# Down products of a Strassen FFN: other order of the PSUM sums, one kept tile W per pair of strips, splits of blocks on VectorE

## The chip, the cores and the metric

The kernel runs on one core of a Trainium2 chip. The metric is the time of one execution in device microseconds. The kernel before took 1813.65 us (median of 3 runs, 1813.53 to 1815.38).

## The reference, cut to what matters

One inference step of a decoder layer with two groups of tokens (1024 prompt tokens and 8 x 4 sample tokens, 1056 columns together) that share all weights: a block of three mixers, cross-attention, and then the part of this case, a SwiGLU feed-forward layer with 2816 hidden rows, and a last RMS norm. All values are fp32.

```
u = rmsnorm(h, W['norm_ffn'][l])
h = h + (jax.nn.silu(u @ W['w_ffn_gate'][l]) * (u @ W['w_ffn_up'][l])) @ W['w_ffn_down'][l]
...
y = rmsnorm(h, W['norm_final'])
```

The change touches only the product with `w_ffn_down`, and of its 22 blocks of 128 hidden rows the first 18. The outputs are h after the last norm, and the states of the mixers.

## The kernel before, in words

Tokens lie along the free dimension: a feature block is a tile of 128 partitions x 1056 columns, cut in two halves of 528 (TH), and each of these in two parts c of 264 (HB). A product in fp32 is made of three matmuls: each operand is split into a rounded high part and the rest (hi, lo), and hi·hi, hi·lo and lo·hi are summed in PSUM (L1323 to L1325). ScalarE makes hi by a copy, another engine makes lo by a subtraction.

The three feed-forward products go by a Strassen-Winograd scheme with 7 products instead of 8 (table `PRODUCTS`, L1281; function `strassen`, L1328). The weight side of a product comes from `lefts` (L1221): per pair of output strips, GpSimd makes the sums s1 and s3 (L1244, L1245) and VectorE s2 and s4 (L1246, L1247), and `split_left` splits seven blocks (hi on ScalarE, L1259; lo on VectorE, L1260, tile `wlo`). The right side are the blocks B11, B21, B22, T1 to T4 of the hidden rows. They were written to DRAM by the stage before (`keep`, L1417) and are read back and split by `load_right` (L1359, tile `xd`): hi on ScalarE (L1369), lo on VectorE for two blocks of three and on GpSimd for the third (L1370).

The down product runs over 3 groups g of 6 hidden blocks, and within a group over 4 pairs m of output strips. Each (g, m) has seven products i = 0 to 6, each of 2 parts x 3 blocks x 3 = 18 matmuls. A PSUM tile `st` holds both parts and there are three of them; a (g, m) uses four in turn: G0 takes B11 (i = 0) and then also B21 (i = 2), G1 takes T2 (1) and T3 (3), G2 takes T1 (4) and B22 (6), G3 takes T4 (5). After a product the function `down` (L1543) takes the sum so far out of PSUM: i = 0 is copied by ScalarE into a half of a tile `tm` (L1547), 1 and 3 are added to it by VectorE (L1549, L1554), 2, 4, 5 and 6 are added straight into h (L1552, L1558, L1560, L1562). GpSimd adds the sums in `tm` to h12 (after 1, L1550), h22 and h21 (after 3, L1555, L1556). A later product that goes into the same PSUM tile has to wait until the reader before it is done.

The 63 blocks of the right side do not come evenly. `feed` (L1405) loads and splits 23 of them around the last products of the stage before, and then 3 after each product of m = 3, for the next group; the split stands three products (6 ticks) later in the program. In group 2, and from the last of m = 3 in group 1 on, `feed` brings the operands of the last four hidden blocks instead (`hl`, L1389; `wd`, L1400).

TensorE's and SyncE's work stands in the order of the program. That of VectorE, ScalarE and GpSimd is put in order by the scheduler, which goes by its own costs; each engine then works through its list in order, so an instruction waits for those ahead of it too.

Of the kernel before, what the change touches and what calls it, by code (L numbers as in the profile page):

```python
# [26 lines left out]
NG, GK = 3, 3  # L27
# [32 lines left out]
def hybrid_step(ctx, tc, xT, memT, consts_d, masks_d, wbd_d, poolw_d, spool_d, w_kv, w_xbc, w_dt, w_lg, w_pool, w_z, h0_d,  # L60
# [1252 lines left out]
    ps_ = ExitStack()  # L1313
    ps = ps_.enter_context(tc.tile_pool(name="ps2", bufs=2, space=PSUM, reuse_waits="tile"))

    def product(i, w, G, c, kk, k0=0):
        xb, g, begins = PRODUCTS[i]
        whi, wlo = w
        for k in range(kk):
            a, b = k * P, k * P + P  # L1320
            xh, xl = X[xb, k0 + k, c]
            out = G[g][:, c, :HB]
            nc.tensor.matmul(out, whi[:, a:b], xh, start=begins and k == 0, stop=False, skip_group_check=True)  # L1323
            nc.tensor.matmul(out, whi[:, a:b], xl, start=False, stop=False, skip_group_check=True)  # L1324
            nc.tensor.matmul(out, wlo[:, a:b], xh, start=False, stop=k == kk - 1, skip_group_check=True)  # L1325
        tick()

    def strassen(kk, after, by_part=False, k0=0):  # L1328

        G = {}  # L1330
        if by_part:
# [8 lines left out]
                G = {}  # L1340
            return
        for i in range(7):
            g = PRODUCTS[i][1]
            if g not in G:
                G[g] = ps.tile([P, 2, 512], F32, tag="st", name=nm("st"), bufs=3)
            w = block()
            for c in range(2):
                product(i, w, G, c, kk, k0)
            after(i, slice(0, 2), G)

    def temps():
# [7 lines left out]
    def load_right(wait):  # L1359
        b, f = next(rights)  # L1360
        t = slot(F32R, "xd")
        hi, lo = t[:, :TH], t[:, TH:]
        nc.sync.dma_start(lo.bitcast(F32), hid_dram[:, f, NB8.index(b)])
        eng = nc.gpsimd if len(hids) % 3 == 2 else nc.vector
        hids.append(t)

        def split():
            yield wait
            nc.scalar.activation(hi, lo.bitcast(F32), AF.Copy)  # L1369
            eng.tensor_tensor(lo, lo.bitcast(F32), hi.bitcast(F32), op=OP.subtract)  # L1370
            for c in range(2):
                X[b, 4 + f, c] = hi[:, c * HB:(c + 1) * HB], lo[:, c * HB:(c + 1) * HB]

        spawn(split())
# [153 lines left out]
        spawn(keep(f, ga, (v22, v12, v21, v11)))  # L1528


    for g in range(NG):
        for m in range(4):
            if g == 0 and m < 3:
# [1 line left out]
                    load_h(i)  # L1535
            if (g, m) == (0, 0):
                feed(2)
            t = slot(name="tm")
            u3, u2 = [t[:, i * TH:(i + 1) * TH].rearrange("p (c t) -> p c t", c=2) for i in range(2)]
            (h11, h12), (h21, h22) = [[x[:, i * TH:(i + 1) * TH].rearrange("p (c t) -> p c t", c=2) for i in range(2)]  # L1540
                                      for x in h[2 * m:2 * m + 2]]

            def down(i, cs, G):  # L1543
                at = lambda g: G[g][:, cs, :HB]
                vec, gp = nc.vector.tensor_tensor, nc.gpsimd.tensor_tensor
                if i == 0:
                    nc.scalar.activation(u3, at(0), AF.Copy)  # L1547
                elif i == 1:
                    vec(u2, u3, at(1), op=add)  # L1549
                    gp(h12, h12, u2, op=add)  # L1550
                elif i == 2:
                    vec(h11, h11, at(0), op=add)  # L1552
                elif i == 3:
                    vec(u3, u3, at(1), op=add)  # L1554
                    gp(h22, h22, u3, op=add)  # L1555
                    gp(h21, h21, u3, op=add)  # L1556
                elif i == 4:
                    vec(h22, h22, at(2), op=add)  # L1558
                elif i == 5:
                    vec(h21, h21, at(3), op=add)  # L1560
                else:
                    vec(h12, h12, at(2), op=add)  # L1562
                if m == 3:
                    feed(3)

            strassen(GK, down, k0=4 + g * GK)
    while tail:
        spawn(tail.pop(0)())
    drain()
# [161 lines left out]
```

## Time and profile before

| what | value |
|---|---|
| median of 3 runs | 1813.65 us |
| time of the profiled execution | 1811.17 us |
| its span in the profile | 1809.3 us |
| TensorE busy | 1727.7 us (95%) |
| VectorE busy | 1181.0 us (65%) |
| ScalarE busy | 780.8 us (43%) |
| GpSimd busy | 704.7 us (39%) |

The span is the stretch from the first to the last recorded instruction; the execution is 1.9 us longer. The down products lie from about 1525 to 1744 us after the span's start. Shares are means over stages with different limits, so the rows below are taken from that stage alone.

### The profile page before, as it was taken

To read this page: it belongs to the slowest core of one execution; us is meant where nothing else is said; L and a number is where in the kernel's file an instruction comes from. 1 tells how busy PE (TensorE), PEld (TensorE's weight loads), DVE (VectorE), ACT (ScalarE), POOL (GpSimd) and SP (SyncE) were. 2 spreads that over 40 slices of the span, in tenths; PEclk is the share of its full clock that TensorE was granted. 3 is DMA by queue.
4 is the path that set the end of the run, shared out by engine and by line. 5 is a ranking of instruction groups with operands and counts; after the bars stand their busy time and mean duration, and the time that the engine had idled before them with its cause. 6 is when DMAs were issued, how large, how long until landed. Compare 5 with 4: busy or idle time off the path is not lost.

```text
span 1809.3 us, 31919 instructions
## 1 busy us (share of the span) xinstructions
PE 1727.7 (95%) x12307; PEld 1674.3 (93%) x12307; DVE 1181.0 (65%) x2112; ACT 780.8 (43%) x1533; POOL 704.7 (39%) x695
## 2 busy tenths in 40 slices
PE   8899999999999999999999999999999998989897
PEld 7798988888999999999999989999999998989896
DVE  5888997788753534455566488555555557798755
ACT  6544544467744213345564364322222224244244
POOL 2423556665342322211221243433344424465534
PEclk9999999999999999999999999999999999999998
DMA  9111222241230522243344232222222237245122
GB/s 345 62 55 60 67 67 87 95 148 61 101 111 32 207 83 84 78 144 124 116 139 146 95 131 72 103 93 95 90 90 101 92 110 264 91 153 166 32 83 97
DMA packets 106504, 197.52 MB, mean 109 GB/s; under 512 B 15344, under 2 KB 33392, under 8 KB 106352
## 3 DMA queue, kind: packets, MB, share of 16 engines
q1 hardware_dynamic: 94832, 173.54, 28.4%
q10 hardware_dynamic: 11520, 21.94, 3.3%
q8 instruction: 97, 1.59, 0.4%
q14 instruction: 55, 0.45, 0.1%
HBM read 151.54 MB, written 43.89 MB: 108 GB/s over the span
## 4 chain that ended last, share of the span: by engine, by line
PE 76%; DVE 12%; issue 4%; POOL 3%; DMA 2%; ACT 2%; ACTq 0%; SPq 0%; DVEq 0%; POOLq 0%
PE mm L153 11%; PE mm L155 11%; PE mm L154 11%; PE st L1323 10%; PE st L1324 10%; PE st L1325 10%; DVE cy L504 2%; DVE wlo L1260 1%; PE poa L1083 1%; DVE xd L1370 1%; PE pss L1065 1%; POOL seg L576 1%; DVE x L331 1%; PE st L1452 1%; PE st L1453 1%
## 5 line engine op out<-in xcount | busy, mean ns | idle before, releaser
L1323 PE MATMUL st<-x,whi 128*128 128x264 f32 x1120 | 319.0, 285 | 3.0 <-DVE tm L1512 1.9
L153 PE MATMUL mm<-uh,whi 128*128 128x352 f32 x960 | 320.7, 334 | 0.0
L1324 PE MATMUL st<-x,whi 128*128 128x264 f32 x1120 | 318.1, 284 | 0.0
L1325 PE MATMUL st<-x,wlo 128*128 128x264 f32 x1120 | 318.0, 284 | 0.0
L155 PE MATMUL mm<-uh,wlo 128*128 128x352 f32 x960 | 310.8, 324 | 0.0
L154 PE MATMUL mm<-ul,whi 128*128 128x352 f32 x960 | 310.8, 324 | 0.0
L1323 PEld LDWEIGHTS st<-x,whi 128*128 128x128 f32 x1120 | 210.7, 188 | 3.6 <-DVE tm L1512 2.1
L1325 PEld LDWEIGHTS st<-x,wlo 128*128 128x128 f32 x1120 | 210.7, 188 | 0.0
L1324 PEld LDWEIGHTS st<-x,whi 128*128 128x128 f32 x1120 | 210.6, 188 | 0.0
L153 PEld LDWEIGHTS mm<-uh,whi 128*128 128x128 f32 x960 | 181.7, 189 | 4.5 <-issue 2.2
L154 PEld LDWEIGHTS mm<-ul,whi 128*128 128x128 f32 x960 | 182.2, 190 | 2.5
L155 PEld LDWEIGHTS mm<-uh,wlo 128*128 128x128 f32 x960 | 181.5, 189 | 0.0
L1323 PE MATMUL st<-xd,whi 128*128 128x264 f32 x504 | 148.5, 295 | 22.7 <-DVE h L1558 12.5
L1324 PE MATMUL st<-xd,whi 128*128 128x264 f32 x504 | 147.1, 292 | 0.0
L1325 PE MATMUL st<-xd,wlo 128*128 128x264 f32 x504 | 147.0, 292 | 0.0
L1259 ACT ACTIVATE whi<-as 128x512 fp32r<-128x512 f32 (+1 forms) x128 | 74.7, 584 | 152.4 <-PE st L1324 101.6
L1259 ACT ACTIVATE whi<-ar 128x512 fp32r<-128x512 f32 (+1 forms) x104 | 60.9, 588 | 151.8 <-PE st L1324 81.3
L123 ACT ACTIVATE whi<-wraw 128x512 fp32r<-128x512 f32 x128 | 78.0, 626 | 104.4 <-PE mm L154 72.4
L1323 PEld LDWEIGHTS st<-xd,whi 128*128 128x128 f32 x504 | 98.5, 195 | 25.6 <-DVE h L1558 11.3
L1260 DVE TENSOR_TENSOR wlo<-as,whi 128x512 fp32r<-128x512 f32 (+1 forms) x128 | 116.0, 907 | 0.0
L958 POOL TENSOR_TENSOR kvlo<-kvraw,kvhi 128x512 fp32r<-128x512 f32 x32 | 41.4, 1295 | 163.9 <-ACT kvhi L957 129.6
L1324 PEld LDWEIGHTS st<-xd,whi 128*128 128x128 f32 x504 | 98.8, 196 | 0.0
(468 smaller groups left out, 4499.1 us busy)
## 6 DMA issues: line engine op xcount, KB each, us to landing
ar<-w_gu SPq DMA_DIRECT2D x88, 256.0 KB, 4.1
hid_dram<-tm SPq DMA_DIRECT2D x71, 264.0 KB, 2.2
xd<-hid_dram SPq DMA_DIRECT2D x63, 264.0 KB, 4.8
ar<-w_down SPq DMA_DIRECT2D x48, 192.0 KB, 3.0
h_dram<-h ACTq DMA_DIRECT2D x16, 528.0 KB, 3.0
h<-h_dram SPq DMA_DIRECT2D x16, 528.0 KB, 6.3
seg<-acs_dram SPq DMA_DIRECT2D x32, 256.0 KB, 3.8
wraw<-w_out SPq DMA_DIRECT2D x32, 256.0 KB, 3.6
```

Source lines behind the costliest of these rows:

```text
L123: nc.scalar.activation(hi[:, a:b], raw, AF.Copy)
L153: nc.tensor.matmul(out, whi[:, a:b], xh[:, cols], start=k == 0, stop=False)
L154: nc.tensor.matmul(out, whi[:, a:b], xl[:, cols], start=False, stop=False)
L155: nc.tensor.matmul(out, wlo[:, a:b], xh[:, cols], start=False, stop=k == kk - 1)
L331: nc.vector.scalar_tensor_tensor(x, x, cc("gmix", k), rb0[:, ch(c)], op0=OP.mult, op1=OP.mult)
L504: nc.vector.scalar_tensor_tensor(y[:, :n], raw[:, j:j + n], w[j], y[:, :n], op0=OP.mult, op1=OP.add)
L958: eng.tensor_tensor(lo, src, hi.bitcast(F32), op=OP.subtract)
L1259: nc.scalar.activation(hi[:, a], src, AF.Copy)
L1260: nc.vector.tensor_tensor(lo[:, a], src, hi[:, a].bitcast(F32), op=OP.subtract)
L1323: nc.tensor.matmul(out, whi[:, a:b], xh, start=begins and k == 0, stop=False, skip_group_check=True)
L1324: nc.tensor.matmul(out, whi[:, a:b], xl, start=False, stop=False, skip_group_check=True)
L1325: nc.tensor.matmul(out, wlo[:, a:b], xh, start=False, stop=k == kk - 1, skip_group_check=True)
```

## The change

The products run in another assignment to PSUM tiles (table `DOWN`): T3 no longer goes into T2's tile but opens a new one (G2), T4 is added to T3 there, T1 opens G3, and B22 is added to T1. `down` no longer builds sums in a tile `tm` for each (g, m). Where g = 0, B11 is copied by ScalarE into a part W[m] of a tile that is kept over the three groups; for g = 1 and 2, VectorE adds it to W[m]. T2 is added to W[m] too, by VectorE. T3 and T1 are added to h22 straight from PSUM, T3 + T4 to h21, T1 + B22 to h12, B11 + B21 to h11. In group 2, after T2, GpSimd adds W[m] to h22, h21 and h12. So VectorE has 6 sums from PSUM per (g, m) in group 0, as before, and 7 in groups 1 and 2; ScalarE has 4 copies instead of 12, GpSimd 12 sums instead of 36. All 63 splits of right-hand blocks are on VectorE; before, 42 were, and 21 on GpSimd.

```diff
--- before.py
+++ after.py
@@ -1313,8 +1313,11 @@
     ps_ = ExitStack()
     ps = ps_.enter_context(tc.tile_pool(name="ps2", bufs=2, space=PSUM, reuse_waits="tile"))
 
-    def product(i, w, G, c, kk, k0=0):
-        xb, g, begins = PRODUCTS[i]
+
+    DOWN = ("B11", 0, True), ("T2", 1, True), ("B21", 0, False), ("T3", 2, True), ("T1", 3, True), ("T4", 2, False), ("B22", 3, False)
+
+    def product(i, w, G, c, kk, k0=0, table=PRODUCTS):
+        xb, g, begins = table[i]
         whi, wlo = w
         for k in range(kk):
             a, b = k * P, k * P + P
@@ -1325,7 +1328,7 @@
             nc.tensor.matmul(out, wlo[:, a:b], xh, start=False, stop=k == kk - 1, skip_group_check=True)
         tick()
 
-    def strassen(kk, after, by_part=False, k0=0):
+    def strassen(kk, after, by_part=False, k0=0, table=PRODUCTS):
 
         G = {}
         if by_part:
@@ -1340,12 +1343,12 @@
                 G = {}
             return
         for i in range(7):
-            g = PRODUCTS[i][1]
+            g = table[i][1]
             if g not in G:
                 G[g] = ps.tile([P, 2, 512], F32, tag="st", name=nm("st"), bufs=3)
             w = block()
             for c in range(2):
-                product(i, w, G, c, kk, k0)
+                product(i, w, G, c, kk, k0, table)
             after(i, slice(0, 2), G)
 
     def temps():
@@ -1361,13 +1364,12 @@
         t = slot(F32R, "xd")
         hi, lo = t[:, :TH], t[:, TH:]
         nc.sync.dma_start(lo.bitcast(F32), hid_dram[:, f, NB8.index(b)])
-        eng = nc.gpsimd if len(hids) % 3 == 2 else nc.vector
         hids.append(t)
 
         def split():
             yield wait
             nc.scalar.activation(hi, lo.bitcast(F32), AF.Copy)
-            eng.tensor_tensor(lo, lo.bitcast(F32), hi.bitcast(F32), op=OP.subtract)
+            nc.vector.tensor_tensor(lo, lo.bitcast(F32), hi.bitcast(F32), op=OP.subtract)
             for c in range(2):
                 X[b, 4 + f, c] = hi[:, c * HB:(c + 1) * HB], lo[:, c * HB:(c + 1) * HB]
 
@@ -1528,6 +1530,8 @@
         spawn(keep(f, ga, (v22, v12, v21, v11)))
 
 
+
+    W = []
     for g in range(NG):
         for m in range(4):
             if g == 0 and m < 3:
@@ -1535,35 +1539,27 @@
                     load_h(i)
             if (g, m) == (0, 0):
                 feed(2)
-            t = slot(name="tm")
-            u3, u2 = [t[:, i * TH:(i + 1) * TH].rearrange("p (c t) -> p c t", c=2) for i in range(2)]
+            if g == 0:
+                if m % 2 == 0:
+                    wt = slot(name="w")
+                W.append(wt[:, m % 2 * TH:m % 2 * TH + TH].rearrange("p (c t) -> p c t", c=2))
             (h11, h12), (h21, h22) = [[x[:, i * TH:(i + 1) * TH].rearrange("p (c t) -> p c t", c=2) for i in range(2)]
                                       for x in h[2 * m:2 * m + 2]]
 
             def down(i, cs, G):
-                at = lambda g: G[g][:, cs, :HB]
-                vec, gp = nc.vector.tensor_tensor, nc.gpsimd.tensor_tensor
-                if i == 0:
-                    nc.scalar.activation(u3, at(0), AF.Copy)
-                elif i == 1:
-                    vec(u2, u3, at(1), op=add)
-                    gp(h12, h12, u2, op=add)
-                elif i == 2:
-                    vec(h11, h11, at(0), op=add)
-                elif i == 3:
-                    vec(u3, u3, at(1), op=add)
-                    gp(h22, h22, u3, op=add)
-                    gp(h21, h21, u3, op=add)
-                elif i == 4:
-                    vec(h22, h22, at(2), op=add)
-                elif i == 5:
-                    vec(h21, h21, at(3), op=add)
+                at = G[DOWN[i][1]][:, cs, :HB]
+                if (g, i) == (0, 0):
+                    nc.scalar.activation(W[m], at, AF.Copy)
                 else:
-                    vec(h12, h12, at(2), op=add)
+                    to = (W[m], W[m], h11, h22, h22, h21, h12)[i]
+                    nc.vector.tensor_tensor(to, to, at, op=add)
+                if g == NG - 1 and i == 1:
+                    for x in (h22, h21, h12):
+                        nc.gpsimd.tensor_tensor(x, x, W[m], op=add)
                 if m == 3:
                     feed(3)
 
-            strassen(GK, down, k0=4 + g * GK)
+            strassen(GK, down, k0=4 + g * GK, table=DOWN)
     while tail:
         spawn(tail.pop(0)())
     drain()
```

What this makes of the engines' lists is shown at two places. The first is VectorE at the passage from group 0 to group 1: from the last weight split ahead of the copy-out of B22 (m = 3) into the first products of group 1. `xd` are splits of right-hand blocks, `wlo` of weight blocks, `as` the weight sums, and `st` a PSUM tile. Before:

```order
L1260 TENSOR_TENSOR wlo2503_17655<-as2484_17540,whi2502_17654 128x384
L1562 TENSOR_TENSOR h2443_17232<-h2443_17232,st2481_17533 128x528
L1260 TENSOR_TENSOR wlo2503_17655<-ar2454_17330,whi2502_17654 128x384
L1260 TENSOR_TENSOR wlo2506_17713<-as2485_17541,whi2505_17712 128x384
L1246 TENSOR_TENSOR as2510_17769<-as2510_17769,ar2482_17534 128x384
L1247 TENSOR_TENSOR as2511_17770<-ar2482_17534,as2510_17769 128x384
L1370 TENSOR_TENSOR xd2489_17579<-xd2489_17579 128x528
L1370 TENSOR_TENSOR xd2490_17581<-xd2490_17581 128x528
L1260 TENSOR_TENSOR wlo2513_17776<-ar2482_17534,whi2512_17775 128x384
L1370 TENSOR_TENSOR xd2493_17611<-xd2493_17611 128x528
L1260 TENSOR_TENSOR wlo2513_17776<-as2510_17769,whi2512_17775 128x384
L1549 TENSOR_TENSOR tm2500_17652<-tm2500_17652,st2504_17685 128x528
```

After the change (`w2407` is W[0] and W[1]; the row with `st2498` takes out B11, that with `st2501` T2):

```order
L1260 TENSOR_TENSOR wlo2500_17640<-as2483_17527,whi2499_17639 128x384
L1260 TENSOR_TENSOR wlo2500_17640<-ar2454_17321,whi2499_17639 128x384
L1372 TENSOR_TENSOR xd2487_17564<-xd2487_17564 128x528
L1372 TENSOR_TENSOR xd2488_17566<-xd2488_17566 128x528
L1372 TENSOR_TENSOR xd2489_17568<-xd2489_17568 128x528
L1555 TENSOR_TENSOR w2407_16842<-w2407_16842,st2498_17638 128x528
L1372 TENSOR_TENSOR xd2490_17595<-xd2490_17595 128x528
L1372 TENSOR_TENSOR xd2491_17597<-xd2491_17597 128x528
L1372 TENSOR_TENSOR xd2492_17599<-xd2492_17599 128x528
L1555 TENSOR_TENSOR w2407_16842<-w2407_16842,st2501_17670 128x528
L1260 TENSOR_TENSOR wlo2503_17697<-as2484_17528,whi2502_17696 128x384
L1372 TENSOR_TENSOR xd2495_17632<-xd2495_17632 128x528
```

Three splits now stand ahead of each copy-out where one to three stood, and the copy of B11, which ScalarE made, is a row of this list.

The second place is the first (g, m) of the down stage. ScalarE before (the row with `tm2407` copies B11):

```order
L1369 ACTIVATE xd2398_16791<-xd2398_16791 128x528
L1259 ACTIVATE whi2419_16983<-ar2364_16554 128x384
L1369 ACTIVATE xd2400_16812<-xd2400_16812 128x528
L1259 ACTIVATE whi2419_16983<-as2417_16977 128x384
L1369 ACTIVATE xd2401_16814<-xd2401_16814 128x528
L1369 ACTIVATE xd2402_16816<-xd2402_16816 128x528
L1547 ACTIVATE tm2407_16842<-st2408_16843 128x528
```

ScalarE after the change (the row with `w2407` copies B11):

```order
L1371 ACTIVATE xd2398_16791<-xd2398_16791 128x528
L1259 ACTIVATE whi2420_16981<-ar2364_16554 128x384
L1371 ACTIVATE xd2400_16812<-xd2400_16812 128x528
L1371 ACTIVATE xd2401_16814<-xd2401_16814 128x528
L1371 ACTIVATE xd2402_16816<-xd2402_16816 128x528
L1259 ACTIVATE whi2420_16981<-as2418_16975 128x384
L1552 ACTIVATE w2407_16842<-st2408_16843 128x528
```

The copy now stands right behind the second half of `whi2420`, which is made from the weight sum `as2418`. That sum is made by VectorE; there it stood ahead of the last two sums of the stage before (`as2417`):

```order
L1246 TENSOR_TENSOR as2417_16977<-as2417_16977,ar2364_16554 128x384
L1518 TENSOR_TENSOR tm2358_16542<-tm2358_16542,st2394_16768 128x264
L1370 TENSOR_TENSOR xd2391_16718<-xd2391_16718 128x528
L1519 TENSOR_TENSOR tm2340_16320<-tm2340_16320,tm2358_16542 128x264
L1370 TENSOR_TENSOR xd2392_16720<-xd2392_16720 128x528
L1260 TENSOR_TENSOR wlo2413_16909<-as2367_16561,whi2412_16908 128x384
L1370 TENSOR_TENSOR xd2396_16787<-xd2396_16787 128x528
```

and after the change it stands behind eight splits of right-hand blocks (`as2418`):

```order
L1521 TENSOR_TENSOR tm2340_16320<-tm2340_16320,tm2358_16542 128x264
L1372 TENSOR_TENSOR xd2392_16720<-xd2392_16720 128x528
L1372 TENSOR_TENSOR xd2387_16698<-xd2387_16698 128x528
L1260 TENSOR_TENSOR wlo2413_16908<-as2367_16561,whi2412_16907 128x384
L1372 TENSOR_TENSOR xd2395_16785<-xd2395_16785 128x528
L1372 TENSOR_TENSOR xd2396_16787<-xd2396_16787 128x528
L1372 TENSOR_TENSOR xd2397_16789<-xd2397_16789 128x528
L1372 TENSOR_TENSOR xd2398_16791<-xd2398_16791 128x528
L1372 TENSOR_TENSOR xd2400_16812<-xd2400_16812 128x528
L1372 TENSOR_TENSOR xd2401_16814<-xd2401_16814 128x528
L1246 TENSOR_TENSOR as2418_16975<-as2418_16975,ar2364_16554 128x384
```

So the first copy of B11 now comes, by way of a weight split, behind these splits of VectorE.

## Rows read from the trace of the kernel before

**Rows 1.** Waits of TensorE, 1480 to 1760 us: in total, times, longest.

```profile
PE st L1323 <- DVE h L1558: 12.5, 5, 3.4
PE st L1323 <- ACT tm L1547: 5.9, 3, 3.0
PE st L1323 <- DVE tm L1549: 4.1, 3, 1.9
```

**Rows 2.** ScalarE in order of time: copies of B11; start, duration, [idle before].

```profile
1531.89 0.59 ACT L1547 ACTIVATE tm<-st 128x528 f32<-128x528 f32 x1
...
1564.52 0.61 ACT L1547 ACTIVATE tm<-st 128x528 f32<-128x528 f32 x1 [1.72 <-PE st L1325]
...
1579.89 0.61 ACT L1547 ACTIVATE tm<-st 128x528 f32<-128x528 f32 x1 [1.72 <-PE st L1325]
...
1603.77 0.59 ACT L1547 ACTIVATE tm<-st 128x528 f32<-128x528 f32 x1
...
1621.77 0.61 ACT L1547 ACTIVATE tm<-st 128x528 f32<-128x528 f32 x1 [1.74 <-PE st L1325]
...
1652.34 0.61 ACT L1547 ACTIVATE tm<-st 128x528 f32<-128x528 f32 x1 [1.74 <-PE st L1325]
...
1675.16 0.59 ACT L1547 ACTIVATE tm<-st 128x528 f32<-128x528 f32 x1
...
1695.54 0.61 ACT L1547 ACTIVATE tm<-st 128x528 f32<-128x528 f32 x1 [2.22 <-PE st L1325]
```

**Rows 3.** Windows: PE, PEld, DVE, ACT, POOL busy, granted clock, DMA.

```profile
1549.20:1564.50 15.30, 15.30 (x128) 15.30 (x127) 10.55 (x16) 3.91 (x8) 7.29 (x5) 1.00 0.37 121
1584.85:1617.03 32.18, 25.45 (x176) 24.30 (x174) 32.14 (x35) 14.96 (x30) 21.67 (x14) 0.89 0.54 181
1657.31:1689.16 31.85, 23.66 (x175) 22.62 (x173) 31.82 (x34) 15.19 (x29) 21.23 (x14) 0.95 0.55 182
1594.80:1597.80 3.00, 3.00 (x15) 3.00 (x15) 3.00 (x4) 0.00 (x0) 1.55 (x1) 0.50 0.96 341
```

**Rows 4.** VectorE by line, 1584.85 to 1617.03 us: busy and mean ns.

```profile
L1370 DVE TENSOR_TENSOR xd<-xd 128x528 fp32r<-128x528 f32 x14 | 17.0, 1250 | 0.0
L1260 DVE TENSOR_TENSOR wlo<-as,whi 128x384 fp32r<-128x384 f32 x6 | 7.5, 1246 | 0.0
L1260 DVE TENSOR_TENSOR wlo<-ar,whi 128x384 fp32r<-128x384 f32 x4 | 3.3, 824 | 0.0
```

**Rows 5.** GpSimd by line, the same stretch.

```profile
L1370 POOL TENSOR_TENSOR xd<-xd 128x528 fp32r<-128x528 f32 x7 | 11.9, 1717 | 0.0
...
L1244 POOL TENSOR_TENSOR as<-ar 128x384 f32<-128x384 f32 x1 | 1.5, 1452 | 3.4 <-ACT xd L1369 3.4
L1245 POOL TENSOR_TENSOR as<-ar,ar 128x384 f32<-128x384 f32 x1 | 1.2, 1201 | 0.6 <-POOL as L1244 0.6
```

**Rows 6.** VectorE in order of time, 1585 to 1625 us.

```profile
1588.98 0.69 DVE L1554 TENSOR_TENSOR tm<-tm,st 128x528 f32<-128x528 f32 x1
1589.60 0.69 DVE L1370 TENSOR_TENSOR xd<-xd 128x528 fp32r<-128x528 f32 x1
1590.22 1.66 DVE L1260 TENSOR_TENSOR wlo<-ar,whi 128x384 fp32r<-128x384 f32 x1
...
1598.69 0.55 DVE L1260 TENSOR_TENSOR wlo<-as,whi 128x384 fp32r<-128x384 f32 x1
1599.16 0.69 DVE L1562 TENSOR_TENSOR h<-h,st 128x528 f32<-128x528 f32 x1
```

**Rows 7.** GpSimd in order of time, at the first of these rows.

```profile
1589.75 1.71 POOL L1555 TENSOR_TENSOR h<-h,tm 128x528 f32<-128x528 f32 x1 [1.87 <-DVE tm L1554]
```

**Rows 8.** VectorE in order of time, around the first (g, m).

```profile
1528.81 0.42 DVE L1519 TENSOR_TENSOR tm<-tm,tm 128x264 f32<-128x264 f32 x1
...
1537.16 0.69 DVE L1549 TENSOR_TENSOR tm<-tm,st 128x528 f32<-128x528 f32 x1
```

**Rows 9.** VectorE in order of time, in the last (g, m).

```profile
1735.42 4.12 DVE L1400 TENSOR_TENSOR wd<-wraw,wd 128x512 fp32r<-128x512 f32 x3
```

## The prediction

> **What bounds the kernel now.** I read the waits of TensorE first, then the pace of the products, then the engine that they wait for. Over the whole kernel TensorE is busy 95% of the span, so there is little to win outside a stage where it waits. In the down stage it waits for readers of PSUM: 12.5 us in five waits for the sum of T1, 5.9 in three for the copy of B11 and 4.1 in three for the sum of T2, 22.5 us together [rows 1]. Each time the next product goes into a PSUM tile whose reader is late.
>
> The pace shows where. The copy of B11 comes once per (g, m). Undisturbed that is 15.37 us (1564.52 to 1579.89) [rows 2]. From m = 3 of group 0 on it is 23.88 and then 18.00 us, 11.1 us over two undisturbed ones; from m = 3 of group 1 on it is 22.82 and 20.38 us, 12.5 us over [rows 2]. I call these bursts A and B. Both are where the splits for the next group come, three per product.
>
> In the bursts VectorE is the engine that is full: busy 32.14 of 32.18 us in A, 31.82 of 31.85 in B, against 10.55 of 15.30 in an undisturbed (g, m) [rows 3]. And it is slow at what it does. The split of a right-hand block takes 0.62 us from start to start when nothing is beside it (1589.60 to 1590.22), a sum from PSUM 0.62 (1588.98 to 1589.60), a weight split 0.47 (1598.69 to 1599.16) [rows 6]. In A the 14 splits took 1250 ns on average, the weight splits 1246 and 824 [rows 4]. The weight split that began at 1590.22 took 1.66 us and ended (1591.88) after GpSimd's sum of 1589.75 to 1591.46 did [rows 6, 7]. So VectorE's operations with both inputs in SBUF stand while GpSimd works; those that read PSUM don't. After a wait the clock can be down as well: 15 matmuls in 3.00 us at a granted 0.50 (the 1.2 GHz level), against 128 in 15.30 us at 1.00 [rows 3]. That is about 1.5 us each time.
>
> **Burst A.** VectorE did 35 operations in 32.14 us [rows 3]: 14 splits, 10 weight splits [rows 4], 2 weight sums and 9 sums from PSUM. Alone they would take 14 x 0.62 + 10 x 0.47 + 2 x 0.5 + 9 x 0.62 = 20.0 us (the two weight sums counted at 0.5 each, near the weight splits, which have the same 384 columns). So 12.1 us went to standing beside GpSimd, which was busy 21.67 us [rows 3]: 0.56 us for each of its microseconds. The change adds the 7 splits that GpSimd did in this stretch (7 x 0.62 = 4.3) [rows 5] and the sum of B11 of the new group (0.62): 25.0 us. GpSimd is left with its two weight sums, 1.5 + 1.2 = 2.7 us [rows 5], since its 7 splits (11.9 us) and its sums into h go. At 0.56 that costs 1.5 us, at nothing 0, at the full 2.7 us 2.7. VectorE's work then is 26.5 us (25.0 to 27.7), 5.6 less (4.4 to 7.1). As VectorE sets the pace in this stretch, the 11.1 us shrink by as much, if no new wait comes. One does: T1 opens a tile that is free only when the sum into h11 is out, and one product lies between B21 and T1 (2.2 us, a seventh of 15.37). In the new list that sum stands behind three splits. I take 1 us back for it (0 to 3). Term A: -4.5, bounds -7 to -1.
>
> **Burst B** has the same shape: 34 operations, 31.82 us, GpSimd 21.23 us [rows 3]. Alone they are 19.9 us (12 splits, 10 weight splits, 2 weight sums, 9 sums, and one `hl`, of twice the columns, at 1.2), so again 11.9 us went beside GpSimd. Added are again 7 splits and one sum, 5.0 us: 24.9. But in group 2 GpSimd adds W to three parts of h, right after T2: three sums at the 1.7 us of rows 7, 5.1 us, and the weight sums, 2.7 as in A. At 0.56 these 7.8 us cost 4.4, so 29.3, 2.5 less than now; with a share of 0 it is 6.9 less, with 1 0.9 more. For T1's tile I take 0.5 here (0 to 2), since B has 19 splits, not 21 (63 less 23 less 21). Term B: -2, bounds -6.9 to +2.9.
>
> **The first (g, m).** T3 opens a tile of its own, so it no longer waits for the sum of T2: one of the three waits of 4.1 us, about 1.5, goes here [rows 1]. Against it: the copy of B11 now comes behind the second half of a weight strip, which comes from a weight sum that VectorE makes after eight splits and a weight split, 8 x 0.62 + 0.47 = 5.4 us, behind the last product of the stage before (1528.81 + 0.42) [rows 8]. That gives 1534.7 for the start of the sum, 1535.2 for its end, and with the weight split and the copy on ScalarE (0.5 and 0.6) about 1536.3, where the copy now ends at 1532.5 [rows 2]: 3.8 us late, if VectorE reaches this place no sooner. It should, by the splits that no longer stand beside GpSimd's. From there VectorE took 8.35 us to the sum of T2 (1528.81 to 1537.16) for 9 operations that alone are 5.1 [rows 8]; the new list has 14 that alone are 8.1, so the sum of T2 comes about as now. Term: -1, bounds -3.5 (T3's wait goes and two of the 3.0 us for the copy, the longest of its waits [rows 1]) to +3.8 (the copy is late in full).
>
> **The last (g, m).** One of the five waits for T1's sum is behind three splits of `wd`, 4.12 us [rows 9], where three at the pace of the others would be under 2; GpSimd's sums into h22 and h21 ran beside them. GpSimd's sums into these now start two products earlier, after T2. The wait (12.5 us in five, the longest 3.4) [rows 1] goes mostly; but `hl` is split in the same place. Term: -2, bounds -4 to +1.
>
> **Edits that cost nothing.** In m = 1 and 2 of each group VectorE is idle 4.75 of 15.30 us [rows 3]; the added sum of 0.62 us in groups 1 and 2 fits, and with GpSimd's three sums in group 2, 5.1 us at 0.56, it is 3.5 us in all, still inside; without that slack each of these (g, m) would lose the rest. ScalarE's eight copies that go (0.6 us each) free nothing that is waited for. Loads keep their order on SyncE's queue.
>
> The Trainium skill, SBUF — State Buffer, section "Who interferes with whom", says that a VectorE operation with two SBUF inputs contends with a GpSimd operation that reads SBUF, as an exclusive lock. By that rule taken in full the share would be 1, and the two bursts would gain 4.6 us less; the trace shows 0.56, since VectorE's sums from PSUM run beside GpSimd in the same stretch.
>
> **Sum.** -4.5 - 2 - 1 - 2 = -9.5 us, on the profiled execution (1811.17 us) as on the median (1813.65), which lie 0.14% apart; I give it on the median: 1804.2 us.
>
> **Rivals.**
> No change that can be told (within 0.2%, 3.6 us, about what a measurement of this kernel can tell): VectorE is still full in the bursts, since 21 splits and 8 sums come to it (18 us alone) and the waits only change their names: A -2, the others nothing: 1812. For it: VectorE has 25 us of work against 21 us of products in each burst, so it stays the limit. Against: the 24 us beside GpSimd in the two bursts.
>
> Slower, by one mechanism: reads of PSUM late in the new order. T1's tile waits for the sum into h11 behind three splits in each burst, and the first copy waits behind eight. It decides if VectorE comes to these sums later than one product (2.2 us) after their matmuls. Price: the sum into h11 comes three splits, a weight split and a stand of 1.7 us after its matmuls (1.9 + 0.5 + 1.7 = 4.1), 1.9 beyond the 2.2, and so does that of T1, for which B22 waits: 3.8 us in each burst. That leaves A at -5.6 + 3.8 = -1.8 and B at -2.5 + 3.8 = +1.3; with the first copy in full (+3.8) and the last (g, m) at its bound (+1) it is +4.3: 1818 us. For it: the order rows. Against: the splits ahead of these sums no longer stand beside GpSimd's, so three of them are 1.9 us, not 3.8 (3 x 1.25).
>
> Much faster: VectorE runs ahead, and all waits go, 22.5 us and some five stretches of low clock at 1.5 us: 30 us, 1783.7. Against it is the 25 us of work in 21.
>
> Slower by crowding: a full engine gets 21 splits more and GpSimd's absence gives nothing back: 21 x 0.62 = 13 us, 1827. Against it: a weight split takes 0.55 us alone and 1.66 beside GpSimd [rows 6]. The Trainium skill, Perfetto Trace Analysis, section "Optimizing Scalar/DVE Operations", says that if VectorE is saturated, offloading to GpSimd may make sense; this change does the reverse. The same section warns that the two share a port, and the trace sides with the warning.
>
> **Chances.** Forecast 0.58; no change 0.18; slower by late reads 0.15; slower by crowding 0.05; much faster 0.04. So faster by over 0.2% 0.62, within 0.2% 0.18, slower 0.20. The forecast's own range is 1797 to 1810. For eight times in ten I take in the case of no change and part of the late reads: 1795 to 1816.
>
> **What would show it.** Right: splits in both bursts at a mean under 0.8 us; from copy-out to copy-out of B11 some 37.4 us in A (23.88 + 18.00 = 41.9 now) and 41.2 in B (43.2 now); waits of TensorE in the stage at half or less; GpSimd nearly idle in A. Burst A gains more than B. Wrong: a first copy of B11 well after its product with TensorE standing over 4 us; T1 as the product that waits longest in A; splits over 1 us though GpSimd is idle.

## The result and the profile after

The changed kernel takes 1795.49 us (median of 4 runs, 1793.21 to 1799.23), the kernel before 1814.52 us beside it (4 runs, 1813.53 to 1817.36). The ratio is 0.9895, with a 95% interval of 0.9873 to 0.9916: 19 us faster. The forecast was 1804.2 us. The direction and the mechanism came out, the size is double the forecast. The measured time lies outside the range of the forecast itself (1797 to 1810 us) and only 0.5 us inside the one given for eight times in ten (1795 to 1816 us). So the question of this part is which terms were too small. The profiled execution took 1793.21 us against 1811.17, 18.0 us less.

To set the two traces side by side I divide the down stage at events that are not late in either kernel. Here are the sums of T2 of m = 1 (groups 1 and 2), which come right after their product, and the first matmul of the tail, first of the kernel before (the columns are start, duration, [idle before]):

```profile
1624.02 0.70 DVE L1549 TENSOR_TENSOR tm<-tm,st 128x528 f32<-128x528 f32 x1 [1.61 <-PE st L1325]
...
1697.79 0.70 DVE L1549 TENSOR_TENSOR tm<-tm,st 128x528 f32<-128x528 f32 x1 [3.07 <-PE st L1325]
...
1743.40 0.53 PE L153 MATMUL mm<-hh,wd 128*128 128x384 f32 x1
```

and of the changed kernel, with its last copy of B11 (m = 3 of group 0) ahead of them:

```profile
1582.51 0.61 ACT L1552 ACTIVATE w<-st 128x528 f32<-128x528 f32 x1 [1.72 <-PE st L1328]
...
1617.90 0.70 DVE L1555 TENSOR_TENSOR w<-w,st 128x528 f32<-128x528 f32 x1 [0.66 <-PE st L1328]
...
1684.13 0.70 DVE L1555 TENSOR_TENSOR w<-w,st 128x528 f32<-128x528 f32 x1 [0.75 <-PE st L1328]
...
1726.46 0.34 PE L153 MATMUL mm<-hh,wd 128*128 128x384 f32 x1
```

With the copy of 1579.89 in [rows 2] that makes:

| stretch | before | after | difference | forecast (bounds) |
|---|---|---|---|---|
| burst A: that copy to T2, m = 1, group 1 | 44.13 | 35.39 | -8.7 | -4.5 (-7 to -1) |
| burst B: from there to T2, m = 1, group 2 | 73.77 | 66.23 | -7.5 | -2 (-6.9 to +2.9) |
| the rest of group 2, to the tail | 45.61 | 42.33 | -3.3 | -2 (-4 to +1) |
| first (g, m): last stage's half copy at 1502.51 or 1505.55 to the copy of m = 3 | 77.38 | 76.96 | -0.4 | -1 (-3.5 to +3.8) |

The four make -19.9. The tail is 1.0 us shorter, and all that lies ahead of the stage, which the change does not touch, took 3.0 us longer in this execution. A and B are the two terms to explain; both lie outside their own bounds.

TensorE's waits, 1480 to 1760 us of the changed kernel, to be set against [rows 1] (total, times, longest):

```profile
PE st L1326 <- ACT w L1552: 6.5, 1, 6.5
PE st L1326 <- DVE h L1555: 2.4, 3, 1.6
PE st L1326 <- DVE w L1555: 1.7, 1, 1.7
PE st L1326 <- ACT xd L1371: 1.5, 1, 1.5
PE st L1326 <- ACT whi L1259: 0.9, 1, 0.9
```

The 12.5 us for T1's sum are gone. What is left is one long wait of 6.5 us, for the first copy of B11, and small ones.

Now the bursts, each from the start of the sum of T2 of m = 3 to the end of the sum of T1 of the next group's m = 0, as windows (us, then PE, PEld, DVE, ACT and POOL busy with instructions, granted clock, DMA share, GB/s). The kernel before, A and B, and then TensorE's 57 matmuls from the end of this stretch to the sum of T2, in B and in A:

```profile
1582.15:1617.03 34.88, 28.14 (x198) 27.00 (x196) 34.84 (x37) 17.66 (x35) 23.59 (x15) 0.90 0.57 190
1654.59:1689.16 34.57, 26.38 (x198) 25.34 (x196) 34.53 (x36) 17.91 (x34) 23.16 (x15) 0.95 0.58 193
...
1689.31:1697.79 8.48, 8.48 (x57) 8.48 (x58) 3.93 (x7) 1.32 (x3) 2.93 (x3) 0.80 0.22 70
1617.09:1624.02 6.93, 6.93 (x57) 6.93 (x58) 3.84 (x8) 1.39 (x4) 3.04 (x3) 1.00 0.26 86
```

The changed kernel, A and B:

```profile
1584.77:1610.93 26.16, 24.40 (x198) 23.89 (x196) 26.10 (x44) 17.05 (x32) 4.32 (x2) 1.00 0.71 256
1648.54:1677.14 28.60, 24.48 (x198) 23.90 (x196) 28.36 (x43) 17.89 (x33) 9.62 (x5) 1.00 0.67 235
```

VectorE is full in all four (busy 28.36 of 28.60 us at the least). Its stretch is 8.72 us shorter in A, and A as a whole 8.74. In B it is 5.97 shorter; the other 1.57 stand in the third row of the first of the two fences: after the last wait of B the same 57 matmuls took 8.48 us at a granted clock of 0.80, where they took 6.93 at 1.00 in A. So VectorE's list explains A almost to the tenth and 6.0 of the 7.5 us of B, and a low clock makes up the rest of B, behind its last wait.

VectorE's lines in A of the changed kernel, and GpSimd's (busy, mean ns), answer [rows 4] and [rows 5]:

```profile
L1372 DVE TENSOR_TENSOR xd<-xd 128x528 fp32r<-128x528 f32 x21 | 14.8, 747 | 0.1
L1555 DVE TENSOR_TENSOR h<-h,st 128x528 f32<-128x528 f32 x8 | 5.5, 694 | 0.0
L1260 DVE TENSOR_TENSOR wlo<-as,whi 128x384 fp32r<-128x384 f32 x5 | 2.7, 548 | 0.0
...
L1244 POOL TENSOR_TENSOR as<-ar 128x384 f32<-128x384 f32 x1 | 3.1, 3052 | 14.8 <-DVE wlo L1260 14.8
L1245 POOL TENSOR_TENSOR as<-ar,ar 128x384 f32<-128x384 f32 x1 | 1.3, 1268 | 3.1 <-DMA ar<-w_down 3.1
```

A split is at 747 ns (1250 before), a weight split at 548 (1246). Now one of GpSimd's two weight sums is stretched: it took 3.05 us beside a full VectorE, 1.45 before.

The first copy, ScalarE in order of time:

```profile
1530.38 1.69 ACT L1371 ACTIVATE xd<-xd 128x528 fp32r<-128x528 f32 x3
1535.43 0.52 ACT L1259 ACTIVATE whi<-as 128x384 fp32r<-128x384 f32 x1 [3.36 <-DVE as L1246]
1535.86 0.59 ACT L1552 ACTIVATE w<-st 128x528 f32<-128x528 f32 x1
```

The copy stands behind a weight half that waits for VectorE's weight sum, as the prediction worked out.

### The profile page after: what moved, and what is told of

It is laid out like the page before. It is cut to its first block, busy times and chain, and to the rows that moved or that the text cites. A ratio compares the mean times of both kernels' runs of the same rounds, so it can differ in the third digit from the quotient of the medians.

```text
span 1791.4 us, 31915 instructions
## 1 busy us (share of the span) xinstructions
PE 1721.7 (96%) x12307; PEld 1669.3 (93%) x12307; DVE 1160.0 (65%) x2141; ACT 778.4 (43%) x1525; POOL 644.0 (36%) x650
## 4 chain that ended last, share of the span: by engine, by line
PE 76%; DVE 12%; issue 4%; POOL 3%; DMA 2%; ACT 2%; SPq 0%; ACTq 0%; DVEq 0%; POOLq 0%
PE mm L153 11%; PE mm L155 11%; PE mm L154 11%; PE st L1326 10%; PE st L1327 10%; PE st L1328 10%; DVE cy L504 2%; PE poa L1083 1%; PE pss L1065 1%; DVE xd L1372 1%; POOL seg L576 1%; DVE x L331 1%; PE st L1454 1%; PE st L1456 1%; PE st L1455 1%
## 5 line engine op out<-in xcount | busy, mean ns | idle before, releaser
L1326 PE MATMUL st<-xd,whi 128*128 128x264 f32 x504 | 144.7, 287 | 13.1 <-ACT w L1552 6.5
L1327 PE MATMUL st<-xd,whi 128*128 128x264 f32 x504 | 144.2, 286 | 0.0
L1244 POOL TENSOR_TENSOR as<-ar 128x512 f32<-128x512 f32 (+1 forms) x32 | 53.3, 1665 | 205.9 <-DVE wlo L1260 174.3
L1326 PEld LDWEIGHTS st<-xd,whi 128*128 128x128 f32 x504 | 95.8, 190 | 14.6 <-ACT w L1552 6.7
L1328 PEld LDWEIGHTS st<-xd,wlo 128*128 128x128 f32 x504 | 95.7, 190 | 0.0
```

The source lines that it names most:

```text
L1244: nc.gpsimd.tensor_tensor(s1, a21, a22, op=OP.add)
```

## The experiments

The theory after the result: what the bursts cost was GpSimd's work on SBUF beside VectorE's operations with two SBUF inputs; the change gains by taking GpSimd's work away. The rivals: the order of the PSUM sums (T3 in a tile of its own) frees TensorE, or the kept W does by fewer operations. VectorE's stretches below run from the sum of T2 to the end of that of T1, as above, each with GpSimd's busy time in it. Each ratio is to runs of the kernel before that stand beside that kernel's own.

| kernel | us | ratio, 95% | VectorE, A / B | GpSimd, A / B |
|---|---|---|---|---|
| before | 1813.65 | | 34.88 / 34.57 | 23.59 / 23.16 |
| changed | 1795.49 | 0.9895 (0.9873 to 0.9916) | 26.16 / 28.60 | 4.32 / 9.62 |
| splits alone | 1811.24 | 0.9980 (0.9965 to 0.9995) | 31.54 / 30.87 | 15.38 / 14.79 |
| order alone | 1813.01 | 0.9995 (0.9985 to 1.0005) | 34.57 / 34.36 | 23.79 / 24.66 |
| order and splits, no kept W | 1808.60 | 0.9968 (0.9952 to 0.9983) | 31.57 / 30.93 | 15.66 / 15.08 |
| order and kept W, no splits | 1804.11 | 0.9940 (0.9922 to 0.9958) | 31.71 / 32.80 | 12.74 / 17.93 |
| old order, splits, GpSimd's sums left out | 1792.43 | 0.9872 (0.9853 to 0.9891) | 25.47 / 24.73 | 5.49 / 4.87 |
| changed, 13 idle sums on GpSimd | 1803.76 | 0.9942 (0.9924 to 0.9960) | 31.05 / 33.11 | 13.78 / 17.88 |
| changed, 6 idle sums | 1799.87 | 0.9919 (0.9898 to 0.9940) | 29.04 / 29.99 | 7.16 / 14.51 |

**The parts of the change.** First the changed kernel with every third split back on GpSimd:

```diff
+        eng = nc.gpsimd if len(hids) % 3 == 2 else nc.vector
...
-            nc.vector.tensor_tensor(lo, lo.bitcast(F32), hi.bitcast(F32), op=OP.subtract)
+            eng.tensor_tensor(lo, lo.bitcast(F32), hi.bitcast(F32), op=OP.subtract)
```

> The changed kernel, but every third split of a right-hand block is on GpSimd again, as before the change. Theory 1 (VectorE stood beside GpSimd's work, 0.56 us for each microsecond of it): GpSimd has some 11.9 us more in each burst, VectorE 7 splits (4.3 us) less, so each burst is some 2.5 to 3.5 us longer than in the changed kernel; the first copy of B11 is no longer behind eight splits, which gives 3 to 4 us back: 1795 to 1800 us in all, with splits at a mean over 1 us in the bursts. Theory 2 (the order of the PSUM sums made the gain): bursts as in the changed kernel, and with the first copy in time 1791 to 1793 us.

1804.11 us: 8.6 us of the gain are gone, and the kernel is slower than either theory's range. VectorE has seven splits fewer in A and its stretch is 5.55 us longer. It is not full there (busy 29.25 of 31.71 us): for the last sums it waits for TensorE.

The kernel before with all splits on VectorE:

```diff
-        eng = nc.gpsimd if len(hids) % 3 == 2 else nc.vector
+        eng = nc.vector
```

> The kernel before with one edit: all splits of right-hand blocks on VectorE. Theory 1: each burst 2 to 3 us shorter, since GpSimd keeps its sums into h; the first copy of B11 about 4 us late, as in the changed kernel: 1811 to 1816 us in all, with the waits at the first copy up and those in the bursts down. Theory 2: the bursts don't gain, and the late first copy makes it 1816 to 1819 us. If the splits alone made the gain of the change, it is under 1802 us.

1811.24 us, in the range of the first theory: 7 x 0.62 = 4.3 us of work came to VectorE in A and its stretch fell by 3.3.

The changed kernel without the kept W: a tile for each (g, m), ScalarE copies B11 in every group, and GpSimd adds W into three parts of h in every (g, m):

```diff
-                if (g, i) == (0, 0):
+                if i == 0:
...
-                if g == NG - 1 and i == 1:
+                if i == 1:
```

> The changed kernel, but W is not kept: each group copies B11 on ScalarE, and GpSimd adds the group's W to h22, h21 and h12 after T2, 36 sums as before the change instead of 12. Theory 1: burst A has some 8 us more of GpSimd, so 3 to 5 us longer than in the changed kernel, burst B 0 to 2: 1799 to 1803 us. Theory 2 (order of the PSUM sums): as the changed kernel, 1794 to 1797 us.

1808.60 us: more is lost than expected by either theory. With 15.66 us of GpSimd's work in A instead of 4.32, VectorE's stretch there is 5.4 us longer, though VectorE has one sum less to make.

The same with the thirds on GpSimd too, so that only the order of the PSUM sums differs from the kernel before:

```diff
+        eng = nc.gpsimd if len(hids) % 3 == 2 else nc.vector
```

> The changed kernel with every third split back on GpSimd and with W anew in each group (GpSimd adds it into three parts of h in every (g, m), as many sums as in the kernel before): so the order of the PSUM sums is changed and GpSimd's work isn't. First theory (GpSimd's work beside VectorE is the cause): the bursts stay, 1810 to 1816. Second theory (the order, with T3 in a tile of its own, is worth it): 1802 to 1807, with TensorE's waits in the stage a third lower.

1813.01 us, ratio 0.9995: by itself the order is worth nothing, and VectorE's stretches (34.57 and 34.36) are those of before. The parts alone make 0 (order) and -3.5 (splits), order and splits -6, order and kept W -10.6, and all three -19: they don't add up. In each of the four parts GpSimd still works 12.7 to 24.7 us in a burst.

**GpSimd's work apart from the order.** The kernel before with all splits on VectorE and without GpSimd's sums into h:

```diff
-                    gp(h12, h12, u2, op=add)
...
-                    gp(h22, h22, u3, op=add)
-                    gp(h21, h21, u3, op=add)
```

> The kernel before with all splits on VectorE and GpSimd's three sums into h left out of every (g, m): parts of the down product are missing in the output. The order of the PSUM sums is the old one, GpSimd is nearly idle in the bursts. First theory (GpSimd's work): both bursts close as in the changed kernel, A from 44.1 to 35 to 37 us, few matmuls at the low clock there, 1794 to 1800. Second theory (order): T3 still waits for the sum of T2 and T1 for its tile; 1804 to 1810, A at 40 us or more.

1792.43 us. With the old order, where T3 waits for T2's sum, both bursts close: A takes 34.80 us (35.39 in the changed kernel) and B 62.66 (66.23). The two windows of VectorE's stretch:

```profile
1586.89:1612.36 25.47, 23.90 (x197) 23.69 (x196) 25.47 (x43) 17.41 (x33) 5.49 (x2) 1.00 0.73 252
1650.08:1674.81 24.73, 23.69 (x195) 23.47 (x194) 24.73 (x42) 17.30 (x32) 4.87 (x2) 1.00 0.74 261
```

This rules out the order as the cause, and shows the two weight sums of GpSimd that stay as nearly free: VectorE's operations alone make 24.4 us in each. But this kernel also leaves out sums that VectorE's own sums into h have to wait for. The next runs leave such waits as they are in the changed kernel.

**A dose of GpSimd's work.** The other way round: nothing of the changed kernel's work is moved, and GpSimd gets idle sums beside every third split of groups 1 and 2.

```diff
+            if extra > 0 and extra % 3 == 2:
+                d = fp.tile([P, TH], F32, tag="dummy", name=nm("dummy"), bufs=1)
+                nc.gpsimd.tensor_tensor(d, hi.bitcast(F32), hi.bitcast(F32), op=add)
```

> The changed kernel, and nothing of its work changed, with a sum on GpSimd added beside every third split of groups 1 and 2 (13 of them, of the split's shape, into a tile that nobody reads). First theory (GpSimd's reading of SBUF beside VectorE is the whole cost): 6 or 7 sums of 1.7 us in each burst, 11 us, stretch VectorE by 0.4 to 0.56 of that, 4.4 to 6.2 us, burst A is back at 40 to 43 us with some 20 to 30 matmuls at the low clock, and B at 70 to 73: 1805 to 1811. Second theory (what counts is how many operations VectorE and the PSUM tiles have to pass): 1794 to 1797.

1803.76 us, 8.3 more than the changed kernel's median and a little below the range of the first theory; the second is out. In A VectorE by line, and the idle sums:

```profile
L1373 DVE TENSOR_TENSOR xd<-xd 128x528 fp32r<-128x528 f32 x21 | 19.3, 959 | 0.2 <-ACT xd L1372 0.2
L1559 DVE TENSOR_TENSOR h<-h,st 128x528 f32<-128x528 f32 x8 | 5.5, 691 | 0.0
...
L1376 POOL TENSOR_TENSOR dummy<-xd 128x528 f32<-128x528 f32 x7 | 9.3, 1329 | 7.7 <-ACT xd L1372 7.5
```

The same 21 splits take 959 ns each instead of 747, and the sums that read PSUM take 691 as they did (694). 9.3 us of idle sums made VectorE's stretch 4.89 us longer, 0.53 per us, and A with it (40.27, +4.88). So GpSimd's work costs this time also where nothing waits for what it makes. With every sixth instead of every third:

> The same with a sum beside every sixth split, 6 in all. If the time goes with VectorE's stretch in proportion: half of what the 13 cost, 1800 to 1803. If the low clock comes in only when waits get long: less than half, VectorE is 2 to 3 us longer in each burst and few matmuls are slow: 1797 to 1800.

1799.87 us, 4.4 more than the changed kernel: about half of 8.3. It lies where the two expected ranges meet, and its runs spread from 1795.68 to 1804.26, so this run does not tell them apart. Three idle sums in A, 4.5 us, made VectorE's stretch 2.88 us longer, 0.64 per us.

**The first copy.** The changed kernel with the first 23 splits in thirds as before, so that VectorE reaches the weight sum earlier:

```diff
+        eng = nc.gpsimd if len(hids) % 3 == 2 and len(hids) < 23 else nc.vector
```

> The changed kernel, but of the first 23 splits (those around the start of the down products) every third is on GpSimd as before the change, the other 40 all on VectorE. In the program's order the first copy of B11 then stands where it stood before. Theory 1: the wait of 6.5 us for the first copy falls to about 3, the bursts stay as in the changed kernel: 1790 to 1793 us. Against it: the wait only moves, to T1's or B22's sum in the first (g, m): 1795 us.

1794.11 us, ratio 0.9886 (0.9867 to 0.9905): not told from the changed kernel. The wait for the copy went from 6.5 to 3.0 us, but not because the copy came sooner. The weight sum did: it began 24.24 us after the half copy of the stage before (29.30 in the changed kernel). The copy began after 31.10 us (30.31), since ScalarE's list now had it behind a weight half that waited for TensorE. TensorE itself came to the wait some 4 us later, in part by a wait of 1.9 us in the stage before that the changed kernel does not have, and the stretch up to the copy of m = 3 took 77.44 us (76.96). Then the weight sum alone, put ahead of the splits:

```diff
-            nc.vector.tensor_tensor(s2, s1, a11, op=OP.subtract)
-            nc.vector.tensor_tensor(s4, a12, s2, op=OP.subtract)
+            with tc.high_priority() if i == NF2 * 2 + 1 else ExitStack():
+                nc.vector.tensor_tensor(s2, s1, a11, op=OP.subtract)
+                nc.vector.tensor_tensor(s4, a12, s2, op=OP.subtract)
```

> The changed kernel with VectorE's two weight sums of the second strip of the down stage put ahead of the seven splits that they stood behind, so that ScalarE's weight half, and the first copy of B11 behind it, are not late. First theory (the copy is late by this one sum, 6.5 us of TensorE's wait and 17 matmuls at the low clock, some 1.8 us): the copy starts near 1532 instead of 1535.9, TensorE's wait goes down to 2 to 3 us, 1790 to 1793. Second theory (VectorE is full there and the wait only moves on to the sums of T2 or B21): the copy is early and TensorE stands later for W or h, 1794 to 1796.

1791.18 us, ratio 0.9871 (0.9855 to 0.9887). ScalarE and TensorE there:

```profile
1530.57 0.51 ACT L1260 ACTIVATE whi<-as 128x384 fp32r<-128x384 f32 x1
1530.98 1.16 ACT L1372 ACTIVATE xd<-xd 128x528 fp32r<-128x528 f32 x2
1532.05 0.59 ACT L1553 ACTIVATE w<-st 128x528 f32<-128x528 f32 x1
...
1532.69 0.39 PE L1327 MATMUL st<-xd,whi 128*128 128x264 f32 x1 [3.00 <-ACT w L1553]
```

The copy starts at 1532.05, not 1535.86, TensorE's wait is 3.0 us, not 6.5, and that stretch takes 73.02 us: 3.9 less, and A, B and the rest are unchanged within 0.1. The interval of the ratio overlaps that of the changed kernel, so the time does not show the gain; the trace says where the 3.9 us are.

**GpSimd in burst B.** W's three sums per (g, m) of group 2 on VectorE:

```diff
-                        nc.gpsimd.tensor_tensor(x, x, W[m], op=add)
+                        nc.vector.tensor_tensor(x, x, W[m], op=add)
```

> The changed kernel, with the three sums of W into h of group 2 on VectorE instead of GpSimd. First theory (GpSimd's work beside VectorE is what the bursts cost; it stretched VectorE by 0.4 to 0.56 us per us): burst B loses 5.6 us of GpSimd's work, worth 2.3 to 3.1 us, and gains three sums at 0.62, 1.9 us, so VectorE is 0.4 to 1.2 us shorter there; the split that took 1.83 us and the `hl` that took 2.37 are back near 0.7 and 1.3; total 1793 to 1796. Second theory (the order of the PSUM sums is what helps, GpSimd costs nothing): VectorE has 1.9 us more in burst B and three sums more ahead of B21's in every (g, m) of group 2: 1797 to 1800.

1793.53 us, ratio 0.9882 (0.9863 to 0.9902): B is 0.5 us shorter, the rest of group 2 0.8 longer, so nothing is won. Both edits together:

> The two edits together that each kept or shortened the time of the changed kernel: the weight sum put early, and W's sums of group 2 on VectorE. If they add up, -4.3 and -2.0 of the two medians: 1788 to 1790. If W's sums on VectorE gave only run to run difference (burst B was 0.5 us shorter and the end 0.8 longer in that trace): the same as the weight sum alone, 1790 to 1792.

1790.63 us, as with the early sum alone, so the two don't add up. Last, the early sum and GpSimd's sums of m = 0 in group 2 issued with those of m = 1:

```diff
+                    late.append((m, h22, h21, h12))
+                    for n, *xs in late if m else []:
...
+                            nc.gpsimd.tensor_tensor(x, x, W[n], op=add)
```

> The weight sum put early, as in the run of that edit alone (1791.2 us), and GpSimd's three sums of W for m = 0 of group 2 issued with those of m = 1, so behind the last sums from PSUM of m = 0. First theory (GpSimd's reading of SBUF in burst B is what keeps B longer than A: VectorE's stretch there is 28.5 us, and 24.7 where GpSimd adds nothing): the 5.6 us of sums leave the burst, VectorE's stretch falls by 0.4 to 0.56 of them, to 25.5 to 26.5 us, B is 2 to 3 us shorter: 1788 to 1790. Second theory (the 19 splits, `hl` and the order of the sums set B): B stays at 66.2 us, or loses where six sums stand together in m = 1: 1790 to 1793.

1791.01 us. VectorE's stretch in B did fall, to 26.26 us with GpSimd at 4.31 in it, as by the first theory, but the time did not: the six sums then stand beside VectorE's weight work of m = 1, and its sum into W is late there:

```profile
1679.05 0.47 PE L1327 MATMUL st<-xd,whi 128*128 128x264 f32 x1 [1.98 <-DVE w L1556]
1679.32 0.42 PE L1328 MATMUL st<-xd,whi 128*128 128x264 f32 x1
```

The wait moved on, with a stretch of low clock behind it (0.42 us a matmul, where it is 0.28). The three versions near 1791 us are the shortest that compute everything.

## Why the prediction was right, and short by half

**What bounds it.** Right: VectorE, by standing beside GpSimd. The share of 0.56 us per us [rows 3, 6, 7] is near what the idle sums cost, 0.53 and 0.64. The Trainium skill, SBUF — State Buffer, section "Who interferes with whom", has it as an exclusive lock. The trace agrees for single operations: a weight split took 1.66 us beside GpSimd's sum and 0.55 alone [rows 6, 7]. The runs also agree that operations with two SBUF inputs alone are touched (splits 747 to 959 ns, sums from PSUM 694 and 691). For a stretch as a whole they give about half. The reason that the text gave for that, VectorE's sums from PSUM beside GpSimd, is not enough: these were 9 x 0.62 = 5.6 us, and 21.67 - 12.1 = 9.6 us of GpSimd's work cost VectorE nothing.

**Burst A, the term that failed most.** The step was "VectorE's work then is 26.5 us, 5.6 less", and a charge of 1 us for T1's tile. The 26.5 was near: the window that I had drawn held 25.5. What was wrong is the start of the window before. I let the burst begin with the first split at 1584.85; it begins with the sum of T2 at 1582.15, and the two weight splits between them took 2.08 us where 0.94 would do, the second 1.61 from start to start beside GpSimd's sum into h12. Counted from sum to sum, VectorE before had 10 sums, 14 splits, 11 weight splits and 2 weight sums, 21.0 us alone, and took 34.88: 13.8 us of standing, not 12.1. After, it is 11 sums, 21 splits, 9 weight splits (two now stand behind T1's sum) and 2 weight sums, 25.1 alone and 1.1 of standing, not 1.5. So 12.7 us of standing went and 4.0 us of work came, which is the 8.7 that were measured.

The charge for T1's tile did not come, and the step behind it, that this tile "is free only when the sum into h11 is out", was wrong. TensorE after its waits in A, and VectorE's sums of B11, T2, and of B21 (into h11) and T3:

```profile
1601.54 0.36 PE L1326 MATMUL st<-xd,whi 128*128 128x264 f32 x1 [1.53 <-ACT xd L1371]
...
1606.00 0.28 PE L1326 MATMUL st<-xd,whi 128*128 128x264 f32 x1
...
1608.59 0.36 PE L1326 MATMUL st<-xd,whi 128*128 128x264 f32 x1 [0.24 <-DVE h L1555]
```

```profile
1600.70 0.69 DVE L1555 TENSOR_TENSOR w<-w,st 128x528 f32<-128x528 f32 x1
...
1603.37 0.69 DVE L1555 TENSOR_TENSOR w<-w,st 128x528 f32<-128x528 f32 x1
...
1607.13 1.31 DVE L1555 TENSOR_TENSOR h<-h,st 128x528 f32<-128x528 f32 x2
```

The product of B21 begins at 1601.54; from there TensorE goes through 54 matmuls, three products, without a wait, so T1's begins at 1606.00, before the sum into h11 (1607.13). Of the three tiles only that of T2 was out by then (its sum began at 1603.37). What TensorE waits for in A is the sum of B11 into W, which ends at 1601.39, and 0.2 us for the sum of T3. The view puts the first of these, 1.5 us, down to ScalarE's half of a split, which ended at about the same time; in the two runs on the first copy the same wait is put down to W.

**Burst B.** The same two errors: 13.6 us of standing before, not 11.9, and 3.6 after, not 4.4; 0.9 for the two weight splits; no charge for T1. With that VectorE's term is -6.0 where I had -2.5. The step that prices GpSimd's work of the changed kernel was near: 9.62 us of it cost 3.6, 0.37 per us. The rest, 1.57, is the low clock behind the last wait, of which the text said "about 1.5 us each time" without making it a term. Inside the bursts the low clock (0.90 and 0.95 before, 1.00 after) was no further cost: VectorE was busy 34.84 of 34.88 and 34.53 of 34.57 us there, so it set the pace, and the slow matmuls only filled time that TensorE would have waited.

**The first (g, m)** came out in its sum (-1 forecast, -0.4), and that is in part luck. The copy is late as worked out, by 0.9 us against the half copy of the stage before rather than 3.8, since VectorE does reach the place sooner. TensorE's wait of 6.5 us, which I had named as a sign of being wrong, takes the place of three of before (3.0, 1.9 and 1.6), so a long wait by itself was a poor sign. Of these three the text had named that of 1.6, for T3; that of 1.9, in the last products of the stage before, it had not. **The last (g, m)**: -3.3, within its bounds; three splits of `wd` take 2.40 us (4.12 in [rows 9]), and from one matmul's start to the next TensorE stands 0.79 us there, 3.28 before.

**The signs.** Splits below 0.8 us, GpSimd nearly idle in A and A ahead of B: seen. From copy-out to copy-out of B11 it is 34.0 us in A and 36.0 in B, where 37.4 and 41.2 were forecast. T1 as the longest wait: not seen. The waits "at half or less": not met, they are 13.0 us against 22.5, and half of them is the first copy.

**The rivals.** Late reads: the first copy came, 0.9 us late; T1's did not, since T1 does not wait for h11. The late reads that came are those of B11 into W (1.5 us in A, 1.7 in B) and of T3 (0.2 and 1.6), inside stretches in which VectorE is full. No change and crowding: out by the ratio. Much faster: more than half of it came. Against it I had "25 us of work in 21"; and VectorE does hold A at 35.4 us, but TensorE at the undisturbed pace would need 33.0 (two times 15.37, and 2.26 from a copy to T2's sum): the two are nearer than I had them.

**What the share hides.** It falls from 0.59 (23.6 us of GpSimd's work in A before) to 0.25 (4.3 us after). The trace has a part of the reason. These are GpSimd's two weight sums, and VectorE's splits beside them:

```profile
1598.59 3.05 POOL L1244 TENSOR_TENSOR as<-ar 128x384 f32<-128x384 f32 x1 [14.79 <-DVE wlo L1260]
1604.76 1.27 POOL L1245 TENSOR_TENSOR as<-ar,ar 128x384 f32<-128x384 f32 x1 [3.12 <-DMA ar<-w_down]
...
1601.32 2.13 DVE L1372 TENSOR_TENSOR xd<-xd 128x528 fp32r<-128x528 f32 x3
...
1604.45 2.76 DVE L1372 TENSOR_TENSOR xd<-xd 128x528 fp32r<-128x528 f32 x3
```

Three splits that nothing disturbs take 1.94 us. Beside the weight sum of 3.05 us VectorE lost 0.2 us, beside that of 1.27 us 0.8. So in the first case it was GpSimd that stood (3.05 us for a sum that takes 1.21 with room), and its standing counts as its busy time. The share is thus no constant that can be carried over. The second idle run shows it too: the 3.05 us weight sum took 1.25 there, so counted by the rise of all of GpSimd's time (7.16 - 4.32 = 2.84 us) its share would be 1.0 instead of 0.64. What decides which of the two engines stands is open.

## What to carry to other kernels

Before an engine is given a term, draw its window from the same event in both kernels, here a sum that is not late, and count what it does between them, the weight splits at the edge too; the first operation that looks like the burst is not where it begins. Where a full VectorE shared a stretch with GpSimd on SBUF, a split on GpSimd saved VectorE 0.62 us and cost it about half of the 1.7 us that GpSimd took, so it was a loss; and the parts that took only some of GpSimd's work out of the bursts gained 3.5 to 10.6 us, where all together gained 19. A low clock cost nothing here while VectorE set the pace, and its full price behind the last wait (57 matmuls in 8.48 us instead of 6.93).

## What the runs showed of the hardware

- GpSimd is stretched too: the same weight sum took 1.21 us beside a VectorE that had time, 1.45 in A before and 3.05 in A after, beside splits without a gap.
- A split on GpSimd took 1.72 us on average in A before and 1.48 with the order and the kept W alone, an idle sum of as many columns 1.33. That this depends on what VectorE does beside it would fit, but is not shown.
- Sums of VectorE that read PSUM kept their 0.69 us in every burst, whatever GpSimd did, while a split of as many columns went from 0.69 us to 1.83 beside it.
